# Turn of layers in a two-layer decoder: order of one evacuation on ScalarE, order of products in a layer's last pair

## The chip, the core and the metric

The kernel runs on one core of a Trainium2 chip. Five engines work side by side, each through its own list of instructions in order: TensorE (PE; its weight loads are shown as PEld), VectorE (DVE), ScalarE (ACT), GpSimd (POOL) and SyncE (SP). They wait for each other through semaphores. PE writes to PSUM, which has eight banks of 128 partitions by 512 float32; the other tiles lie in SBUF. DMAs are issued by SP, POOL and ACT. The metric is the device time of one execution in microseconds (us), the median of several.

## The reference

A decoder trunk of two layers on 512 tokens of 1024 features, all in float32. Each layer mixes (attention over a sliding window beside a retention branch, both gated) and then applies an MLP; the change lies where the MLP of the first layer ends and the second layer begins, and in the MLP's up projection.

```python
def hybrid_layer(x, g_mix, w_in, sinks, w_a, w_b, w_out, g_mlp, w_up, w_down):
    h = rmsnorm(x, g_mix)
    z = h @ w_in
    ...
    x = x + mixed @ w_out

    h2 = rmsnorm(x, g_mlp)
    x = x + jnp.square(jax.nn.relu(h2 @ w_up)) @ w_down
    return x
```

`w_up` is 1024 x 4096, `w_down` 4096 x 1024, `w_in` 1024 x 5888. A final rmsnorm follows the second layer.

## The kernel before

**Products.** A float32 product is made of three products in a rounded float32 format (fp32r): each operand is split into a high part (ACT copies it to fp32r) and a low part (DVE subtracts), and `products` (lines 391 to 393) issues hi·hi, hi·lo and lo·hi. Weights come by SP's queue in units of 128 x 1024 (`raw`), and `split_until` splits them (line 339 on ACT, 340 on DVE) up to three units ahead of their use. In the group that opens the second layer `by_halves` (line 406) issues the same products in another order: all with a unit's high weights, then all with its low weights, then the high weights with the low parts of x.

**The MLP.** The 4096 inner features are taken in eight blocks of 512 (`e` = 0 to 7). A block's up projection is two *pairs* (only block 0 is made otherwise), its down projection is `down` (in the last block of the last layer `down_plain`). Both `pair` and `down` use a block scheme with seven products in place of eight. `pair(which)` computes 256 inner features for 512 tokens; it holds three PSUM banks: a, e and b. Its steps, with their lines:

- a takes four times three products of x's first quarter (line 391 to 393, shown as `mm<-xh,hi` and so on);
- `nc.scalar.activation(b, a, AF.Copy)`, line 1343: ACT copies a into bank b, on which b's products then accumulate;
- e takes twelve products of the first sum (`sums[0]`, shown as `mm<-r,hi`), line 1344; ACT copies it to `eu`, line 1345;
- b goes on with `sums[1]`, is copied to `eu` (1348); a goes on and is evacuated through Relu into `z` (1350); b with `sums[2]` and e with x's last quarter meet `eu` on DVE (1355, 1357); b with `sums[3]` ends in `z` (1363).

Block 7 of the first layer thus has two pairs in a row, 28 pairs stand in the whole program, and the pool `ps_mm` that gives their banks has five. `down` takes four banks of it and two of the second pool, `ps_aux` (b).

**The end of a layer.** `down` writes its results through an object `into`. For blocks 0 to 6 that is `Adding`, which adds to the tensor `y` in DRAM by accumulating DMAs. For block 7 it is `Ending`: it loads `y` back into SBUF and adds the last block there. The layer's output has two token halves, i = 0 and 1. For i = 0 DVE adds from PSUM (`add`). For i = 1 in the first layer `join` does it: ACT evacuates PSUM to a temporary `eu` (line 1515) and a POOL DMA adds it to the tile `y` (line 1516). The last of these four joins is (j, m) = (0, 1); it is the last result of `down`, from bank b.

**The turn.** `y` has tokens on the partitions, x has features there, so the sum is transposed on PE (`turn`, line 1554), four 128 x 128 transposes for a tile, and DVE adds it to x (line 1560). `last_but_one` does the half i = 0, that is x chunks 0 to 3, and splits each chunk with the next layer's gain (`scaled_input`, line 414 on ACT and 415 on DVE). `carry` does i = 1, x chunks 4 to 7, which needs the joins. `squares` squares all eight chunks for the next rmsnorm (ACT, lines 546 and 549; DVE adds, 550; PE sums over the partitions, 562) and stores x to DRAM (`spill`, line 1595, SP's queue). `carry` and `squares` are called from within the first `group` of the second layer, after the high-weight products of its second unit.

**What sets the order.** The program is written through a scheduler (`schedule_with_timeline_sim=True`): when the program is built, it lays out each engine's list by a simulated timeline. Of the instructions that are ready there, the one that stands earlier in the program goes first; tiles and banks are given out in the same pass. On the chip the lists are fixed. `tc.issue_after(ins)` adds to what is written in its block, on the engine of `ins` alone, that it stands behind `ins` in that list; it makes nothing wait for the end of `ins`. `latest[0]` is the last matrix product written so far.

Of the kernel before, what the change touches and what calls it, by code (L numbers as in the profile page):

```python
# [12 lines left out]
AF = mybir.ActivationFunctionType  # L13
# [31 lines left out]
N_BLOCK = 8  # L45
# [70 lines left out]
def decoder(ctx, tc, xT, x_first, w_in, w_rv, w_a, w_b, w_out, w_up, w_pair, w_down, w_end, tables, decay, band, g_last, out):  # L116
    nc = tc.nc
# [13 lines left out]
    def temp(name="t"):  # L131
        return tmp.tile([P, T], F32, tag="t", name=name, bufs=7)

    def big(name, dtype=F32):
        return tmp.tile([P, 2, T], dtype, tag="big", name=name, bufs=6)

    def bank(pool, name):
        return pool.tile([P, T], F32, tag=pool.name, name=name)
# [212 lines left out]
    def unit(name, layer):  # L351
        i = state["next"]
        assert order[i][:2] == (layer, name), (order[i], layer, name)
        state["next"] += 1
        hold = state["hold"]
        split_until(i + SPLIT + 1 if hold is None else max(i + 1, min(hold, i + SPLIT + 1)))
        return parts.pop(i)
# [27 lines left out]
    def products(ps, pairs, start, stop, resume=False):  # L385


        n = len(pairs)
        for i, ((ah, al), (bh, bl)) in enumerate(pairs):
            more = {"skip_group_check": True} if resume else {}  # L390
            nc.tensor.matmul(ps, ah, bh, start=start and i == 0, stop=False, **more)  # L391
            nc.tensor.matmul(ps, ah, bl, start=False, stop=False, **more)  # L392
            latest[0] = nc.tensor.matmul(ps, al, bh, start=False, stop=stop and i == n - 1, **more).ins  # L393

    latest, behind = [None], []
# [148 lines left out]
    def square_sum(acc, src, first):  # L544
        if first:
            nc.scalar.activation(acc, src, AF.Square)
        else:
            sq = temp("sq")
            nc.scalar.activation(sq, src, AF.Square)
            nc.vector.tensor_tensor(acc, acc, sq, ALU.add)  # L550
# [28 lines left out]
    def squared_input(k, which):  # L579
        if k == 0:  # L580
            acc_of[which] = tmp.tile([P, T], F32, tag="acc", name="acc", bufs=1)
        square_sum(acc_of[which], x[:, k, :], k == 0)
# [32 lines left out]
    def layer_body(layer):  # L615
        g_mix, g_mlp = 2 * layer, 2 * layer + 1
# [516 lines left out]
        for u in range(4):  # L1133
            hi, lo = unit("w_a", layer)
            for j in range(2):
                c = 2 * u + j
                ps = bank(ps_mm, "mm")
# [90 lines left out]
        sums = Forms((0, 2))  # L1228
# [47 lines left out]
        def block(half, tokens):  # L1276
            at = slice(tokens * H, tokens * H + H)
            return [(xh[:, k, at], xl[:, k, at]) for k in range(4 * half, 4 * half + 4)]
# [27 lines left out]
        def second_rest(z):  # L1306
            if not kept:
                return
            kept.pop()
            u_forms.rest(0, z, (3,))  # L1310
# [15 lines left out]

            return put

        def pair(which):
            def multiply(ps, weights, left, moving, start=True):  # L1330
                hi, lo = weights
                cols = [slice((0 if left else 4 * P) + k * P, (0 if left else 4 * P) + (k + 1) * P) for k in range(4)]
                products(ps, [((hi[:, c], lo[:, c]), m) for c, m in zip(cols, moving)], start, True, not start)

            a, e, b = (bank(ps_mm, "mm")[:, :H] for _ in range(3))
            eu, z = temp("eu"), big("z")  # L1340
            part = unit("pair", layer)
            multiply(a, part, True, block(0, 0))
            nc.scalar.activation(b, a, AF.Copy)  # L1343
            multiply(e, part, False, sums[0])
            nc.scalar.activation(eu[:, :H], e, AF.Copy)
            part = unit("pair", layer)
            multiply(b, part, True, sums[1], False)
            nc.scalar.activation(eu[:, H:], b, AF.Copy)
            multiply(a, part, False, block(1, 0), False)
            nc.scalar.activation(z[:, 0, :H], a, AF.Relu)  # L1350
            if which:
                second(z, slice(0, 1), SOON)
            part = unit("pair", layer)
            multiply(b, part, True, sums[2], False)
            nc.vector.scalar_tensor_tensor(z[:, 1, H:], b, -1.0, eu[:, :H], ALU.mult, ALU.subtract)
            multiply(e, part, False, block(1, 1), False)
            nc.vector.tensor_tensor(z[:, 0, H:], e, eu[:, H:], ALU.add)
            nc.scalar.activation(z[:, :, H:], z[:, :, H:], AF.Relu)
            if which:
                second_late(z)  # L1360
            part = unit("pair", layer)
            multiply(b, part, True, sums[3], False)
            nc.scalar.activation(z[:, 1, :H], b, AF.Relu, scale=-1.0)
            if which:
                second(z, slice(1, 2), SOON)
                second_rest(z)
            elif plain:
                first_plain(z)
            else:
                first_two(z)  # L1370
# [119 lines left out]
        class Ending:  # L1490
# [21 lines left out]

            def join(self, i, j, m, ps, scale):
                t = temp("eu")
                nc.scalar.activation(t, ps, AF.Copy, scale=scale)
                nc.gpsimd.dma_start(self.y[i, j, m], t, accum_op=ALU.add)

            def add(self, i, j, m, ps, scale, at=slice(0, T)):
# [3 lines left out]
            def put(self, i, j, m, ps, sign, at=slice(0, T)):  # L1522
                block = 2 * j + m
                scale = (factor if sign > 0 else negative)[:, block : block + 1]
                if i and not last:
                    self.join(i, j, m, ps, scale)
                    return
                with tc.issue_after(self.queued) if i else ExitStack():
                    self.add(i, j, m, ps, scale, at)
                if last:  # L1530
                    v = self.y[i, j, m]
                    first, total, both = (sq[:, n * NB + block : n * NB + block + 1] for n in range(3))
                    nc.scalar.activation(temp("junk")[:, at], v[:, at], AF.Square, accum_out=both if i else first)
                    if not i:
                        nc.vector.tensor_tensor(v, v, last_gain[:, i, :], ALU.mult)
                        self.queued = nc.vector.tensor_scalar(first, first, 1.0 / D, EPS, ALU.mult, ALU.add).ins
                        return
                    if at.stop < T:
                        nc.vector.scalar_tensor_tensor(first, both, 1.0 / D, first, ALU.mult, ALU.add)
                        return  # L1540
                    nc.scalar.activation(total, both, AF.Sqrt, bias=first, scale=1.0 / D)
                    nc.vector.reciprocal(total, total)
                    nc.vector.scalar_tensor_tensor(v, v, total, last_gain[:, 1, :], ALU.mult, ALU.mult)
                    nc.sync.dma_start(out[:, block, T:], v)
                    v = self.y[0, j, m]
                    nc.scalar.activation(v, v, AF.Copy, scale=total)
                    nc.scalar.dma_start(out[:, block, :T], v)
# [18 lines left out]
            def last_but_one(self):  # L1566
                if not last:
                    for half in range(2):
                        for j in range(2):
                            turned = self.turn(0, j, half, ps_mm)  # L1570
                        for k in (2 * half, 2 * half + 1):
                            self.behind = scaled_input(k, g_mix + 2)
                        if half == 0:
                            self.turned = turned
                            behind.append(self.behind)
                    behind.append(self.behind)

# [13 lines left out]

            def squares(self):
                for k in range(KD):
                    squared_input(k, g_mix + 2)
                    nc.sync.dma_start(spill[:, k, :], x[:, k, :])

        def first_hooks():
# [16 lines left out]
        for e in range(N_BLOCK):  # L1614
            if e == 0:
                into = Adding(e)
                hooks = first_hooks()
                for c in (0, 2):
                    two_chunks("w_up", layer, xs, [put_up(c), put_up(c + 1)], hooks[c // 2])
            else:  # L1620
                plain = last and e == N_BLOCK - 1
                into = Ending() if e == N_BLOCK - 1 else Adding(e)
                pair(0)
                pair(1)
            if last and e == N_BLOCK - 1:
                down_plain(into)
            else:
                down(e, into)
# [177 lines left out]
```

## Time and profile before

| | |
|---|---|
| time, median of 3 runs | 1468.51 us (1467.56 to 1468.66) |
| the profiled execution | 1466.77 us |
| its span, first to last instruction | 1465.0 us |
| PE busy, of the span | 1453.4 us, 99% |
| DVE busy | 1124.7 us, 77% |
| ACT busy | 944.6 us, 64% |
| POOL busy | 209.0 us, 14% |
| granted TensorE clock | 0.999 |
| DMA | 287.32 MB, 196 GB/s on average |

The profile is of one execution. A row of its timeline has the start in us from the span's beginning, the duration, the engine (a q behind it means its queue), the line of the kernel, the operation, what it writes and reads (`out<-in`), the shapes, and how many like instructions were merged; brackets give the idle time of the engine before it and who ended that. Matrix products overlap: one of 512 columns is shown with 0.39 us though the next starts 0.23 us later. A wait for several semaphores is put down to the one that came last. The row "DMA to landing" gives the time from a DMA's issue until its data is there, as minimum, median and maximum of those in the window that was asked.

### The profile page before, as it was taken

To read this page: it belongs to the slowest core of one execution; us is meant where nothing else is said; L and a number is where in the kernel's file an instruction comes from. 1 tells how busy PE (TensorE), PEld (TensorE's weight loads), DVE (VectorE), ACT (ScalarE), POOL (GpSimd) and SP (SyncE) were. 2 spreads that over 40 slices of the span, in tenths; PEclk is the share of its full clock that TensorE was granted. 3 is DMA by queue.
4 is the path that set the end of the run, shared out by engine and by line. 5 is a ranking of instruction groups with operands and counts; after the bars stand their busy time and mean duration, and the time that the engine had idled before them with its cause. 6 is when DMAs were issued, how large, how long until landed. Compare 5 with 4: busy or idle time off the path is not lost.

```text
span 1465.0 us, 21388 instructions
## 1 busy us (share of the span) xinstructions
PE 1453.4 (99%) x7751; PEld 1256.2 (86%) x7751; DVE 1124.7 (77%) x1697; ACT 944.6 (64%) x1549; POOL 209.0 (14%) x302
## 2 busy tenths in 40 slices
PE   9999999999999999999999999999999999999998
PEld 7888888888889999999878888888888899999996
DVE  6978877866677888888878688787757678888885
ACT  7657556543467777777756575565435777777775
POOL 0111001112001111112201110012110111111120
PEclk9999999999999999999999999999999999999999
DMA  7597349689815767666956973597793377777664
GB/s 263 182 295 207 114 152 259 200 207 290 228 57 193 195 188 199 181 172 188 297 172 191 291 212 104 181 251 189 228 272 101 99 197 199 196 189 199 180 186 140
DMA packets 95867, 287.32 MB, mean 196 GB/s; under 512 B 11152, under 2 KB 11280, under 8 KB 90896
## 3 DMA queue, kind: packets, MB, share of 16 engines
q0 software_dynamic: 33648, 113.26, 34.3%
q1 hardware_dynamic: 61392, 171.37, 33.5%
q8 instruction: 61, 1.00, 0.3%
q10 hardware_dynamic: 720, 1.31, 0.2%
q14 instruction: 46, 0.38, 0.1%
HBM read 246.05 MB, written 107.48 MB: 241 GB/s over the span
## 4 chain that ended last, share of the span: by engine, by line
PE 97%; DMA 1%; ACT 1%; DVE 0%; issue 0%; SPq 0%; DVEq 0%; ACTq 0%
PE mm L391 25%; PE mm L393 25%; PE mm L392 25%; PE b L391 3%; PE b L392 3%; PE b L393 3%; PE rv L391 2%; PE rv L392 2%; PE rv L393 2%; PE mm L406 1%; PE score L774 1%; PE pT L739 1%; PE r L393 1%; PE r L392 1%; PE r L391 1%; DMA y<-eu 1%
## 5 line engine op out<-in xcount | busy, mean ns | idle before, releaser
L339 ACT ACTIVATE hi<-raw 128x1024 fp32r<-128x1024 f32 (+1 forms) x375 | 382.3, 1020 | 285.3 <-PE mm L392 166.0
L340 DVE TENSOR_TENSOR lo<-raw,hi 128x1024 fp32r<-128x1024 f32 (+1 forms) x376 | 439.2, 1174 | 144.6 <-ACT hi L339 143.2
L391 PE MATMUL mm<-xh,hi 128*128 128x512 f32 (+1 forms) x976 | 344.1, 355 | 1.0 <-ACT xh L414 1.0
L392 PE MATMUL mm<-xl,hi 128*128 128x512 f32 (+1 forms) x976 | 344.0, 355 | 0.0
L393 PE MATMUL mm<-xh,lo 128*128 128x512 f32 (+1 forms) x976 | 341.9, 355 | 0.0
L393 PE MATMUL mm<-r,lo 128*128 128x256 f32 (+1 forms) x736 | 239.2, 325 | 0.5 <-DVE lo L340 0.5
L392 PE MATMUL mm<-r,hi 128*128 128x256 f32 (+1 forms) x736 | 239.3, 325 | 0.0
L391 PE MATMUL mm<-r,hi 128*128 128x256 f32 (+1 forms) x736 | 236.6, 325 | 0.5 <-ACT mm L1343 0.5
L391 PEld LDWEIGHTS mm<-xh,hi 128*128 128x128 f32 x976 | 184.8, 189 | 25.6 <-ACT xh L414 1.4
L392 PEld LDWEIGHTS mm<-xl,hi 128*128 128x128 f32 x976 | 184.9, 189 | 24.2
L393 PEld LDWEIGHTS mm<-xh,lo 128*128 128x128 f32 x976 | 183.9, 189 | 23.6
L391 PEld LDWEIGHTS mm<-r,hi 128*128 128x128 f32 x736 | 139.9, 190 | 13.7 <-ACT mm L1343 0.7
L392 PEld LDWEIGHTS mm<-r,hi 128*128 128x128 f32 x736 | 139.9, 190 | 13.2
L393 PEld LDWEIGHTS mm<-r,lo 128*128 128x128 f32 x736 | 139.9, 190 | 12.1 <-DVE lo L340 0.7
L1488 POOL DMA_DIRECT2D y<-eu x56 | 62.4, 1358 | 369.1 <-DVE eu L1473 369.1
L392 PE MATMUL mm<-lo,r 128*128 128x512 f32 (+1 forms) x276 | 104.4, 388 | 0.0
L393 PE MATMUL mm<-hi,r 128*128 128x512 f32 (+1 forms) x276 | 101.2, 387 | 0.0
L391 PE MATMUL mm<-hi,r 128*128 128x512 f32 (+1 forms) x276 | 98.7, 391 | 0.5 <-ACT r L411 0.2
L391 PE MATMUL b<-hi,r 128*128 128x512 f32 x180 | 70.5, 392 | 0.0
L392 PE MATMUL b<-lo,r 128*128 128x512 f32 x180 | 70.3, 391 | 0.0
L393 PE MATMUL b<-hi,r 128*128 128x512 f32 x180 | 67.9, 390 | 0.0
L1488 POOL DMA_DIRECT2D y<-y x56 | 55.6, 1007 | 78.7 <-ACT y L1483 73.5
(299 smaller groups left out, 2382.3 us busy)
## 6 DMA issues: line engine op xcount, KB each, us to landing
raw<-w_in_in SPq DMA_DIRECT2D x73, 512.0 KB, 4.8
sums_down<-w_down_in POOLq DMA_DIRECT2D x30, 1024.0 KB, 11.1
sums_up<-w_pair_in POOLq DMA_DIRECT2D x56, 512.0 KB, 10.2
raw<-w_down_in SPq DMA_DIRECT2D x45, 512.0 KB, 6.8
raw<-w_pair_in SPq DMA_DIRECT2D x84, 256.0 KB, 3.7
y<-y POOLq DMA_DIRECT2D x62, 256.0 KB, 9.0
y<-eu POOLq DMA_DIRECT2D x62, 256.0 KB, 8.1
raw<-sums_down SPq DMA_DIRECT2D x30, 512.0 KB, 7.1
```

The lines of the kernel that those rows point to most:

```text
L339: state["high"] = nc.scalar.activation(hi[:, at], raw[:, at], AF.Copy).ins
L340: nc.vector.tensor_tensor(lo[:, at], raw[:, at], f32(hi[:, at]), ALU.subtract)
L391: nc.tensor.matmul(ps, ah, bh, start=start and i == 0, stop=False, **more)
L392: nc.tensor.matmul(ps, ah, bl, start=False, stop=False, **more)
L393: latest[0] = nc.tensor.matmul(ps, al, bh, start=False, stop=stop and i == n - 1, **more).ins
L406: latest[0] = nc.tensor.matmul(ps, w[:, cols(j, c)], moving[k][low], start=first, stop=bool(final)).ins
L739: nc.tensor.transpose(pt[:, i * P : (i + 1) * P], sm[:, at : at + P], ident)
L774: nc.tensor.matmul(ps[:, g * w : (g + 1) * w], q_s[g][:, c, at], part[:, keys], start=i == 0, stop=i == 1)
L1488: nc.gpsimd.dma_start(y[:, 2 * j + m, i * T : (i + 1) * T], t, **how)
```

## The change

Three edits.

In `pair`, the twelve products of e are written ahead of the copy b<-a, in all 28 pairs. In the second pair of block 7, in both layers, e's products stand behind a's last product in PE's list.

In `Ending`, `join` remembers its evacuation; the last join, (0, 1) of i = 1, is queued on ACT behind `self.ahead`, which is the high part of x chunk 1 (line 414, the first half of `last_but_one`).

In `squares`, each squaring is queued on ACT behind the last join's evacuation. The stores to DRAM beside it stay as they are.

```diff
-        def pair(which):
+        def pair(which, ordered=False):
...
             multiply(a, part, True, block(0, 0))
+            with tc.issue_after(latest[0]) if ordered else ExitStack():
+                multiply(e, part, False, sums[0])
             nc.scalar.activation(b, a, AF.Copy)
-            multiply(e, part, False, sums[0])
             nc.scalar.activation(eu[:, :H], e, AF.Copy)
...
             def join(self, i, j, m, ps, scale):
                 t = temp("eu")
-                nc.scalar.activation(t, ps, AF.Copy, scale=scale)
+                self.joined = nc.scalar.activation(t, ps, AF.Copy, scale=scale).ins
                 nc.gpsimd.dma_start(self.y[i, j, m], t, accum_op=ALU.add)
...
                 if i and not last:
-                    self.join(i, j, m, ps, scale)
+                    with tc.issue_after(self.ahead) if (j, m) == (0, 1) else ExitStack():
+                        self.join(i, j, m, ps, scale)
                     return
...
                             self.turned = turned
+                            self.ahead = self.behind[0]
                             behind.append(self.behind)
...
             def squares(self):
                 for k in range(KD):
-                    squared_input(k, g_mix + 2)
+                    with tc.issue_after(self.joined):
+                        squared_input(k, g_mix + 2)
                     nc.sync.dma_start(spill[:, k, :], x[:, k, :])
...
                 pair(0)
-                pair(1)
+                pair(1, e == N_BLOCK - 1)
```

## The prediction

> **What bounds the kernel now.** I read the page first: span, busy time, the chain that ended last.
>
> ```profile
> span 1465.0 us, 21388 instructions
> PE 1453.4 (99%) x7751; PEld 1256.2 (86%) x7751; DVE 1124.7 (77%) x1697; ACT 944.6 (64%) x1549; POOL 209.0 (14%) x302
> PE 97%; DMA 1%; ACT 1%; DVE 0%; issue 0%; SPq 0%; DVEq 0%; ACTq 0%
> ```
>
> TensorE (PE) is busy for 99% of the span and holds 97% of the chain. The diff adds and removes no matrix product, so it can gain only what PE stands idle, and lose only by new idle time. The view of waits, for PE alone, lists all of it that a wait explains:
>
> ```profile
> PE turn L1554 <- DMA y<-eu: 1.2, 1, 1.2
> PE warm L371 <- DVE ones L366: 1.1, 1, 1.1
> PE mm L391 <- ACT xh L414: 1.0, 1, 1.0
> PE mm L393 <- DVE lo L340: 0.5, 1, 0.5
> PE mm L391 <- ACT mm L1343: 0.5, 1, 0.5
> PE mm L391 <- ACT r L411: 0.2, 1, 0.2
> ```
>
> That is about 4.5 us (1.2+1.1+1.0+0.5+0.5+0.2); the second and third lie in the start (the warm-up and the first products). The diff touches the places of the first, the fifth and the sixth row, and no other. So this is a change of one to three microseconds at best, unless it makes new stalls. 0.2% of the median, 2.94 us, is about what a measurement of this kernel can tell from no change.
>
> **The turn of layers.** The timeline of ScalarE (ACT) and PE, from the last products of layer 0 on (columns: start, duration, engine, line, operation; in brackets the idle time before):
>
> ```profile
> 727.72 0.40 PE L393 MATMUL b<-hi,r 128*128 128x512 f32 x1
> 727.32 1.34 ACT L414 ACTIVATE xh<-x 128x512 fp32r<-128x512 f32 x2 [1.18 <-DVE x L1560]
> 728.56 1.05 ACT L339 ACTIVATE hi<-raw 128x1024 fp32r<-128x1024 f32 x1
> 729.51 0.61 ACT L546 ACTIVATE acc<-x 128x512 f32<-128x512 f32 x1
> 730.03 0.67 ACT L1515 ACTIVATE eu<-b,columns 128x512 f32<-128x512 f32 x1
> 731.05 0.85 POOL L1516 DMA_DIRECT2D y<-eu  x1 [3.71 <-ACT eu L1515]
> 735.47 0.82 PE L1554 MATMUL turn<-ident,y 128*128 128x128 f32 x6
> 736.04 1.63 PE L406 MATMUL mm<-xh,lo 128*128 128x512 f32 x6
> 738.83 0.87 PE L1554 MATMUL turn<-ident,y 128*128 128x128 f32 x6 [1.16 <-DMA y<-eu]
> DMA to landing us min/median/max: 7.7/7.7/7.7
> DMA to landing us min/median/max: 4.6/4.6/4.6
> ```
>
> The last product into the joined block b ends at 728.12 (727.72 + 0.40). ACT is free at 728.66, but then runs a weight split (L339) and the first square (L546), and evacuates b only at 730.03. The accumulating DMA is issued at 731.05 and lands 7.7 us later (first landing row), at about 738.8. PE takes six transposes at 735.47, six products, and waits 1.16 us for that landing. The last row is the landing of the join's DMA before it, issued at 726.5: 4.6 us.
>
> The diff queues the squares behind this evacuation, and the evacuation behind the split of x chunk 1, the second of the two L414 at 727.32. It has no edge for the weight split; its description says that the evacuation goes ahead of one. So the evacuation moves up by 0.52 us (730.03 − 729.51, the square alone) to 1.47 us (730.03 − 728.56, both). I take 1.47, for the evacuation stands earlier in the program than that split and b is complete 0.54 us before ACT is free. With it moves the one DMA that it feeds (L1516); POOL had been idle 3.71 us before it, so it passes nothing in that queue. SP's queue has no part in it: the spill writes read x, not the squares.
>
> What is late next costs nothing, by these rows:
>
> ```profile
> 730.25 1.22 DVE L340 TENSOR_TENSOR lo<-raw,hi 128x1024 fp32r<-128x1024 f32 x1
> 733.65 1.98 PE L406 MATMUL mm<-xh,hi 128*128 128x512 f32 x8
> 747.88 1.49 DVE L550 TENSOR_TENSOR acc<-acc,sq 128x512 f32<-128x512 f32 x2
> 754.14 0.95 PE L562 MATMUL ssq<-ones,acc 128*128 128x1 f32 x8
> ```
>
> The split and the square start about 0.6 us later (the evacuation's 0.67 less overlap). The split ends by 730.3 instead of 729.61, and PE uses that second weight unit from 733.65 on: 3 us of cover. The sum of squares is complete at 749.37 and is read at 754.14: 4.8 us of cover. Were that cover gone, each would cost the 0.6 us.
>
> What the earlier landing is worth: issued at 729.58, the DMA lands at 734.2 with the 4.6 us of its neighbour, at 737.3 with its own 7.7 us. PE comes to the waiting transposes at 737.67 (736.04 + 1.63) in today's order; the order is written when the program is built, so it may put them up to the six products (1.63 us) earlier, at 736.04. In most of these pairings landing comes before arrival, so the 1.16 us go; I count **1.2 us**. Bounds: 0 (landing at 737.3 with arrival at 736.04 leaves 1.26 us, as much as now) and 1.4, counted by starts (738.83 − 736.04, less six steps of 0.23).
>
> [...]
>
> **The last pair of layer 0.** Second pair, block 7:
>
> ```profile
> 694.64 1.06 ACT L339 ACTIVATE hi<-raw 128x1024 fp32r<-128x1024 f32 x1 [1.99 <-PE mm L392]
> 696.02 0.37 ACT L1343 ACTIVATE mm<-mm 128x256 f32<-128x256 f32 x1 [0.33 <-PE mm L393]
> 696.30 0.38 ACT L1350 ACTIVATE z<-mm 128x256 f32<-128x256 f32 x1
> 701.90 0.37 ACT L1345 ACTIVATE eu<-mm 128x256 f32<-128x256 f32 x1
> 695.71 0.28 PE L393 MATMUL mm<-xh,lo 128*128 128x256 f32 x1
> 696.44 0.39 PE L391 MATMUL mm<-r,hi 128*128 128x256 f32 x1 [0.46 <-ACT mm L1343]
> 696.67 0.28 PE L392 MATMUL mm<-r,hi 128*128 128x256 f32 x1
> 705.05 0.28 PE L393 MATMUL mm<-xh,lo 128*128 128x256 f32 x1
> 705.51 0.50 PE L391 MATMUL mm<-hi,r 128*128 128x512 f32 x1 [0.18 <-ACT r L411]
> 705.85 0.39 PE L392 MATMUL mm<-lo,r 128*128 128x512 f32 x1
> ```
>
> The copy b<-a (L1343) starts the moment a's products end, and PE waits for it with b's products: from 695.71 to 696.67 there are 0.96 us where two steps of 0.12 would do (1425.28 to 1425.40 in the last fence), so **0.72 us** lost. e's products, which need nothing from ACT, came later: their evacuation (L1345) is at 701.90. The five PSUM banks explain it: the pair before holds three, a the fourth, and the copy, first in the program, the fifth; e waited for the bank that L1350 empties at 696.30. The diff puts e's products before the copy in the program (all 28 pairs) and, in the last pair of each layer, behind a's on PE. Then e holds the fifth bank and its twelve products (12 × 0.12 = 1.44 us) cover the copy, if L1350 empties a bank for it in time: L1350 and L1343 together are 0.75 us. Bounds: 0.72 gained, or 0.72 lost once more if L1350 is queued behind a's end; I take 0.72, as ACT idles 1.99 us just before.
>
> Moving e's products forward also brings the twelve products behind them nearer. At 705.51 the down stage waits for the split of the first pair's result, from 705.05 to 705.85: 0.80 where 0.12 + 0.23 would do (six 512-column products in 1.63 us at 736.04, the last one 0.4 long, step by 0.23 to 0.25), **0.45 us**. PE would arrive there 0.72 us earlier, but the result of the first pair is finished up to 1.44 us earlier; I count the 0.45 as gone, bounds 0 and 0.45.
>
> In the last layer the same pair has no gap: a's last product at 1425.28, the next at 1425.40, the copy beside it. There, and in the other pairs, the copy was covered already, so I cost the edit at nothing:
>
> ```profile
> 1425.28 0.28 PE L393 MATMUL mm<-xh,lo 128*128 128x256 f32 x1
> 1425.40 0.28 PE L391 MATMUL mm<-r,hi 128*128 128x256 f32 x1
> 1425.69 0.36 ACT L1343 ACTIVATE mm<-mm 128x256 f32<-128x256 f32 x1
> 574.79 0.36 ACT L1350 ACTIVATE z<-mm 128x256 f32<-128x256 f32 x1
> 578.36 0.36 ACT L1343 ACTIVATE mm<-mm 128x256 f32<-128x256 f32 x1
> ```
>
> **Sum.** 1.2 + 0.72 + 0.45 = 2.37 us off. The profiled execution took 1466.77 us, its span 1465.0 and 1.77 around it; the span becomes 1462.6. The median of the runs, 1468.51, lies 1.74 above that execution, so I forecast 1468.51 − 2.37 = 1466.1 us.
>
> **Rivals.**
> 1. *The turn keeps its wait.* The planner moves the transposes forward with the evacuation, and landing and arrival shift alike. For it: bounds above meet at 1.26 us. Against it: a quieter neighbour lands in 4.6. Only the pair's 1.17 us remain: 1467.3.
> 2. *The change does not do what it says*: other work takes the slot on ACT, the pair's bank is late; the order of PE stays as it is: 1468.5.
> 3. *The landing does not move* (slower). If traffic and not issue decides the 738.8, and the transposes are planned 1.63 us earlier, PE stands from 736.04 to 738.83, 2.8 us instead of 1.4; with the pair's gain lost too, 1469.9. It decides from a transfer of 9.2 us (738.8 − 729.58) on; the longest of the join's rows is 7.7.
> 4. *The bank* (slower). If in the other second pairs too b's copy gets its bank only after e's products, each loses the 0.72 us: 14 × 0.72 = 10.1, less 1.2 at the turn, 1477.4. It decides when L1343 starts over 1.44 us after a's end. Against it: at block 3 L1350 empties a bank at 574.79, 3.2 us before the copy (578.36 − 575.15).
> 5. *More falls away*: planned anew, layer 1 loses its 0.5 us wait (fourth row of waits) as well: 1465.5 or below.
>
> **How the numbers follow.** Forecast 0.46, rivals 0.20, 0.09, 0.07, 0.12 and 0.06 in order. The runs of before differ by 1.1 us (1467.56 to 1468.66), so about a quarter of the forecast's share falls beyond −2.94 us: faster 0.11 + 0.06 = 0.17; slower 0.12, the bank alone; same the remaining 0.71. The range goes from 1465.0 (rival 5 and half the scatter) to 1470.0 (rival 3) and leaves out the bank and a few hundredths.
>
> **What would show it.** Right: the L1515 at the turn directly behind the two L414 and ahead of L546; its DMA landing before PE comes to the second transposes; no entry for L1554, L1343 or that L411 in PE's waits; L1345 of layer 0's last pair near 697.5. Wrong: PE's wait on the join's DMA still over 1 us (rival 1 or 3), a new wait of PE on L1343 in several pairs (rival 4), or new PE waits in layer 1, whose order is planned anew from the turn on; that last is what I can price least.

## The result, and the profile after

The changed kernel took 1473.45 us (median, 1470.51 to 1474.58) beside 1468.03 us (1466.12 to 1468.87) for the kernel before on the same chip: 1.0037 times as long, 95% interval 1.0024 to 1.0050. It is slower, by about 5 us; 1466.1 us had been forecast.

The page of the changed kernel. Its execution took 1474.58 us, 7.8 us more than the 1466.77 us of before's:

```profile
span 1472.8 us, 21340 instructions
...
PE 1457.5 (99%) x7751; PEld 1258.8 (85%) x7751; DVE 1122.7 (76%) x1697; ACT 943.5 (64%) x1549; POOL 208.8 (14%) x302
...
PE 97%; ACT 1%; DMA 1%; DVE 0%; issue 0%; SPq 0%; DVEq 0%; ACTq 0%
```

PE has the same 7751 products, yet is "busy" for 4.1 us longer: some of them ran slower. The rest is waiting. PE's waits follow (what it waited for, total, times, longest). Lines behind the edits have numbers one to four higher than before: L1343 is L1345, L1345 is L1346, L1515 is L1516, L1554 is L1556.

```profile
PE mm L406 <- ACT xh L414: 2.7, 1, 2.7
PE mm L393 <- DVE lo L340: 1.8, 1, 1.8
PE warm L371 <- DVE ones L366: 1.1, 1, 1.1
PE mm L391 <- ACT r L411: 1.0, 2, 0.8
PE mm L391 <- ACT eu L1346: 0.9, 1, 0.9
PE mm L391 <- ACT xh L414: 0.8, 1, 0.8
```

Against before: the wait on the join's DMA (1.2) is gone, as forecast. New is 2.7 us at the turn, where PE waits for ACT's split of x (L414). L340 grew by 1.3, L411 by 0.8 (one wait of 0.81 us at 1449.75, in the last layer), and 0.5 on the copy became 0.9 on e's evacuation; the wait in the start is 0.2 shorter. That is 3.8 us. The two places where products ran slower are in the windows (busy time and count of each engine; the last three columns are PEclk, DMA share, GB/s). Before:

```profile
6.00:8.00 2.00, 2.00 (x11) 1.63 (x10) 2.00 (x4) 2.00 (x5) 0.00 (x0) 1.00 0.92 319
8.00:10.00 2.00, 2.00 (x11) 1.65 (x10) 2.00 (x5) 2.00 (x5) 0.00 (x0) 1.00 1.05 388
...
735.00:740.00 5.00, 3.84 (x23) 3.02 (x22) 4.40 (x6) 1.34 (x2) 0.00 (x0) 1.00 0.97 304
```

After:

```profile
6.00:8.00 2.00, 2.00 (x6) 1.52 (x6) 2.00 (x4) 1.77 (x4) 0.00 (x0) 1.00 0.95 309
8.00:10.00 2.00, 2.00 (x6) 1.60 (x5) 1.84 (x4) 1.75 (x4) 0.00 (x0) 1.00 1.05 406
...
730.00:735.00 5.00, 2.33 (x10) 1.72 (x9) 4.26 (x6) 2.71 (x4) 0.45 (x1) 0.88 0.96 265
735.00:740.00 5.00, 5.00 (x18) 4.03 (x18) 4.75 (x6) 5.00 (x9) 0.40 (x1) 0.78 0.92 270
```

At the turn the granted clock falls: 5 x 0.12 + 5 x 0.22 = 1.7 us lost. In windows of 1 us it stands at 0.50 from 734 to 737. In the start six products pass in 2 us where eleven did before, in two rows: ten fewer, at 0.227 us each 2.3 us. Together 3.8 + 1.7 + 2.3 = 7.8 us, all of it. The start is not the change's: PE's list is the same up to about 458 us, and a second profile of the changed kernel (e5, below) has the start as before.

**The turn.** First PE before, around its transposes of the first token half:

```profile
720.46 0.40 PE L393 MATMUL mm<-hi,r 128*128 128x512 f32 x1
720.70 0.60 PE L1554 MATMUL turn<-ident,late 128*128 128x128 f32 x4
...
725.25 1.47 PE L1554 MATMUL turn<-ident,late 128*128 128x128 f32 x12
```

Then PE, DVE and ACT after:

```profile
725.30 0.62 PE L393 MATMUL mm<-hi,r 128*128 128x512 f32 x2
...
728.25 0.40 PE L393 MATMUL b<-hi,r 128*128 128x512 f32 x1
728.49 1.91 PE L1556 MATMUL turn<-ident,late 128*128 128x128 f32 x16
733.06 3.20 PE L406 MATMUL mm<-xh,hi 128*128 128x512 f32 x8 [2.67 <-ACT xh L414]
...
725.73 1.41 DVE L1521 SCALAR_TENSOR_TENSOR late<-mm,columns,late 128x512 f32<-128x512 f32 x2 [0.94 <-PE mm L393]
729.23 0.69 DVE L1562 TENSOR_TENSOR x<-x,turn 128x512 f32<-128x512 f32 x1 [2.09 <-PE turn L1556]
729.84 1.22 DVE L340 TENSOR_TENSOR lo<-raw,hi 128x1024 fp32r<-128x1024 f32 x1
730.97 1.88 DVE L1562 TENSOR_TENSOR x<-x,turn 128x512 f32<-128x512 f32 x3
...
732.28 1.34 ACT L414 ACTIVATE xh<-x 128x512 fp32r<-128x512 f32 x2 [4.28 <-DVE x L1562]
733.53 0.67 ACT L1516 ACTIVATE eu<-b,columns 128x512 f32<-128x512 f32 x1
734.10 1.05 ACT L339 ACTIVATE hi<-raw 128x1024 fp32r<-128x1024 f32 x1
```

Before, four transposes went right behind another bank's last product (720.46), eighteen products of b followed, then the other twelve transposes and six more products of b to cover the sums and splits. After, all sixteen stand behind b's last product (728.25): nothing is left to run while DVE adds and ACT splits, and PE stands idle for 2.67 us. Part of that time DVE spends on a weight split (L340 at 729.84, 1.22 us) between its first add to x and the other three; before, the split (727.20) came behind the first three adds. No run moved this split alone, so its share of the gap is not shown. The eight products at 733.06 take 3.20 us where seven steps of 0.227 and the last one's 0.39 would make 2.0. The join's evacuation (L1516 at 733.53) is where the diff says, right behind the two L414 and ahead of L339.

### The profile page after: what moved, and what is told of

The parts are those of the page before. It is cut to its first block, busy times and chain, and to the rows that moved or that the text cites. A ratio compares the mean times of both kernels' runs of the same rounds, so it can differ in the third digit from the quotient of the medians.

```text
span 1472.8 us, 21340 instructions
## 1 busy us (share of the span) xinstructions
PE 1457.5 (99%) x7751; PEld 1258.8 (85%) x7751; DVE 1122.7 (76%) x1697; ACT 943.5 (64%) x1549; POOL 208.8 (14%) x302
## 4 chain that ended last, share of the span: by engine, by line
PE 97%; ACT 1%; DMA 1%; DVE 0%; issue 0%; SPq 0%; DVEq 0%; ACTq 0%
PE mm L391 25%; PE mm L392 25%; PE mm L393 25%; PE b L391 3%; PE b L392 3%; PE b L393 3%; PE rv L393 2%; PE rv L391 2%; PE rv L392 2%; PE mm L406 2%; PE score L774 1%; PE pT L739 1%; PE r L393 1%; PE r L392 1%; PE r L391 1%; DMA raw<-sums_up 0%
## 5 line engine op out<-in xcount | busy, mean ns | idle before, releaser
L339 ACT ACTIVATE hi<-raw 128x1024 fp32r<-128x1024 f32 (+1 forms) x375 | 383.0, 1022 | 292.3 <-PE mm L392 185.8
L340 DVE TENSOR_TENSOR lo<-raw,hi 128x1024 fp32r<-128x1024 f32 (+1 forms) x376 | 439.5, 1174 | 158.4 <-ACT hi L339 157.3
```

The lines of the kernel that those rows point to most:

```text
L339: state["high"] = nc.scalar.activation(hi[:, at], raw[:, at], AF.Copy).ins
L340: nc.vector.tensor_tensor(lo[:, at], raw[:, at], f32(hi[:, at]), ALU.subtract)
```

## The experiments

Each kernel was run beside the kernel before on the same chip. Times are medians in us; the ratio has its 95% interval. The largest wait is PE's in each profile, start and the wait on L340 apart.

| run | time | before | ratio | largest wait of PE |
|---|---|---|---|---|
| e1 turn's edits alone | 1466.40 | 1466.54 | 1.0000 (0.9991 to 1.0008) | 0.46, block 7 |
| e2 pairs' edits alone | 1480.98 | 1466.54 | 1.0096 (1.0082 to 1.0110) | 6.36 at 861; turn 2.66 |
| e3 b in the other pool | 1471.60 | 1466.54 | 1.0038 (1.0024 to 1.0052) | 3.49, block 7 |
| e4 last pairs and turn | 1469.90 | 1466.54 | 1.0020 (1.0011 to 1.0030) | 1.79, block 7 |
| e5 the change again | 1473.10 | 1466.91 | 1.0039 (1.0027 to 1.0052) | 2.66, turn |
| e6 transposes sooner | 1470.57 | 1466.91 | 1.0026 (1.0016 to 1.0035) | 1.28, turn |
| e7 gap filled | 1469.08 | 1466.91 | 1.0018 (1.0010 to 1.0027) | 0.88, block 7 |
| e8 last pair, second layer | 1466.77 | 1466.91 | 0.9999 (0.9990 to 1.0008) | 0.81, last `down` |
| e9 all but last pairs | 1472.57 | 1466.62 | 1.0030 (1.0019 to 1.0042) | 2.25, block 7 |
| e10 no pin | 1472.78 | 1466.62 | 1.0040 (1.0027 to 1.0054) | 2.66, turn |
| e11 transposes first | 1471.36 | 1466.62 | 1.0029 (1.0017 to 1.0040) | 1.21, turn |
| e12 last pair, first layer | 1468.89 | 1466.62 | 1.0012 (1.0004 to 1.0021) | 1.79, block 7 |
| e13 not in blocks 7 | 1467.08 | 1466.98 | 0.9998 (0.9989 to 1.0008) | 0.46, block 7 |
| e14 second layer only | 1468.72 | 1466.98 | 1.0011 (1.0002 to 1.0020) | 0.81, last `down` |

"Block 7" is that of the first layer. The medians of the kernel before lie between 1466.54 and 1468.03, and the speed of the first products, which changes by execution (last section), moves single profiles by about 2 us. So profiles with the same start are compared too.

### Which part of the diff

Theory A put the loss on the pairs' edit and the shortage of banks, its variant A2 on e's move in every pair; theory B put it on the evacuation that is queued behind the split of x.

e1, the turn's edits without the pairs':

```diff
-            with tc.issue_after(latest[0]) if ordered else ExitStack():
-                multiply(e, part, False, sums[0])
-            nc.scalar.activation(b, a, AF.Copy)
+            with ExitStack():
+                nc.scalar.activation(b, a, AF.Copy)
+            multiply(e, part, False, sums[0])
```

> The edits at the turn alone; the copy b<-a stands ahead of e's products as in the kernel before. The lists of all engines are then those of before but for one swap on ACT: the last join's evacuation ahead of the first square (not ahead of the weight split). Theory A (the pairs' order costs the time): PE's wait for the join's DMA falls from 1.16 us by the square's 0.52 to about 0.6, no other new wait; ratio to before 0.999 to 1.000. Theory B (queueing the evacuation behind the split of x costs the time): 3 us or more lost at the turn, ratio 1.002 or above.

1.0000: no loss, and no gain that can be measured. Its ACT and PE:

```profile
730.68 1.05 ACT L339 ACTIVATE hi<-raw 128x1024 fp32r<-128x1024 f32 x1
731.64 0.67 ACT L1516 ACTIVATE eu<-b,columns 128x512 f32<-128x512 f32 x1
732.20 0.62 ACT L546 ACTIVATE acc<-x 128x512 f32<-128x512 f32 x1
...
740.22 0.87 PE L1556 MATMUL turn<-ident,y 128*128 128x128 f32 x6 [0.41 <-DMA y<-eu]
```

The evacuation passes the square only, not the weight split: 0.52 us of the 1.47 I had taken. Its DMA took 7.5 us (before 7.7). So the wait shrinks by 0.75 us, to 0.41, and does not go.

e2, the pairs' edits without the turn's:

```diff
-                    with tc.issue_after(self.ahead) if (j, m) == (0, 1) else ExitStack():
+                    with ExitStack():
                         self.join(i, j, m, ps, scale)
...
-                    with tc.issue_after(self.joined):
+                    with ExitStack():
                         squared_input(k, g_mix + 2)
```

> e's products ahead of the copy in all pairs, and behind a's in the last ones; the turn's edits are out. Theory A: PE idle of 0.9 us in block 7's last pair and of about 2.7 us at the turn stay, ratio as with the whole change, 1.0025 to 1.005. Theory B: the 2.7 us at the turn go, since the evacuation no longer waits for the split of x; ratio below 1.002.

Much slower still. The 2.66 us at the turn are there without any of the turn's edits, behind the same sixteen transposes, so B falls. What e2 loses beyond the changed kernel is in the second layer (the rows from 840.85 on):

```profile
726.52 1.91 PE L1556 MATMUL turn<-ident,late 128*128 128x128 f32 x16
731.10 3.49 PE L406 MATMUL mm<-xh,hi 128*128 128x512 f32 x8 [2.66 <-ACT xh L414]
...
840.85 0.33 SPq L195 DMA_DIRECT2D raw<-w_a_in  x1
841.23 0.61 SPq L626 DMA_DIRECT2D rawtab<-tables_in  x1
...
858.83 1.23 DVE L627 TENSOR_TENSOR tab<-rawtab,rstd 128x1024 f32<-128x1024 f32 x1 [8.04 <-DMA rawtab<-tables_in]
...
860.94 0.76 PE L391 MATMUL mm<-xh,hi 128*128 128x512 f32 x1 [6.36 <-DVE rot L636]
```

A table load (L626) is issued at 841.23, right behind a weight load in SP's list; before it was issued at 825.39. DVE waits 8.04 us for its data, and PE 6.36 us for DVE.

e3, b of the first layer's last pair in the second pool of banks, so that the copy needs no bank of e's pool:

```diff
-            a, e, b = (bank(ps_mm, "mm")[:, :H] for _ in range(3))
+            a, e, b = (bank(pool, "mm")[:, :H] for pool in (ps_mm, ps_mm, ps_aux if ordered and not last else ps_mm))
```

> The whole change, but in the last pair of the first layer b lies in a bank of the second pool, so the copy needs no bank that the Relu of the pair before must empty first. Theory A: PE's wait of 0.9 us in that pair goes, the pair's results come some 2 us earlier, products of b stand behind the turn's transposes again, and the idle at the turn falls from 2.7 us to under 1; 3 to 4 us of the loss go, ratio 0.9995 to 1.0015. Theory B: the turn keeps its 2.7 us, ratio 1.003 or above.

The loss stays. The wait in the pair goes, as A expected, and PE no longer waits at the turn for more than 0.2 us. But it now waits 3.49 us in front of `down` in block 7 (for r L411): with other banks the lists are laid out anew, and the stall has moved.

e4 has e moved in the last pairs of both layers only, with the turn's edits; e12 in the first layer's last pair alone (`ordered and not last` in place of `ordered`); e8 in the second layer's alone (`ordered and last`). The diff is e4's:

```diff
+            if not ordered:
+                nc.scalar.activation(b, a, AF.Copy)
             with tc.issue_after(latest[0]) if ordered else ExitStack():
                 multiply(e, part, False, sums[0])
-            nc.scalar.activation(b, a, AF.Copy)
+            if ordered:
+                nc.scalar.activation(b, a, AF.Copy)
```

> The turn's edits, and e's products ahead of the copy in the last pair of each layer alone; the other 26 pairs as before. Theory A: the wait in block 7's last pair stays near 0.9 us or less, as the bank is short there alone; how much of the turn's 2.7 us stays depends on how many of b's products stand behind the transposes (12 here, none in the changed kernel), I expect under 1 us; ratio 0.9995 to 1.0015. A rival A2 (moving e costs in every pair): this one is as fast as before within 0.5 us and the changed kernel's loss lies spread over the blocks. Theory B: 1.003.

> The turn's edits, and e's products ahead of the copy only in the last pair of the first layer (pinned there as in the changed kernel). The run with both last pairs moved had 1.79 us of PE idle in this pair, on a DVE instruction (L1359 there) that stands behind two weight splits, 0.88 us before it, and 0.81 us before the last down stage. Theory T: the first two are this pair's and stay, the third goes back to 0.13 us; about 0.7 us under that run's 1469.9, so 1469.2. Rival: the pair's waits are scatter and go; 1466.5 to 1467.

> The turn's edits as in the changed kernel, and e's products ahead of the copy only in the last pair of the second layer (twelve lines of PE's list differ from the kernel with the turn's edits alone). Theory T: everything as with the turn's edits alone but the wait on r L411 in front of the last down stage, 0.81 us in all four profiles with that pair moved, 0.13 us in the two without; so 0.6 to 0.8 us slower than the kernel with the turn's edits alone, whose median was 1466.4: 1467.1. Rival: the 0.7 us is made up behind it (the last stage is short of other work), 1466.4 and the same as before.

The waits of e4 and e12 in block 7 are alike: both have 0.88 us on e's evacuation and 1.79 us on DVE, 2.0 us more than before's 0.46 and 0.18. PE in e12:

```profile
707.71 0.39 PE L391 MATMUL mm<-r,hi 128*128 128x256 f32 x1 [1.79 <-DVE z L1359]
```

The wait before the last `down` is 0.81 us in e4 and 0.13 in e12, and e12's 1468.89 us lie near the 1469.2 expected. At the turn PE waits 0.5 us in e4 and 0.2 in e12, in place of 1.2. So e4 lay above what A expected, and by another wait as well, the 1.79 us on DVE. A2 had e4 within 0.5 us of before, and it falls too. e12 shows more: with the edit only in the one pair whose wait on the copy was to go (and the turn's edits, which cost nothing in e1), the kernel is slower (1.0012). e8's trace has the 0.81 us; its time does not show it, and with an interval 0.0018 wide it could not.

### The order at the turn, and the clock

Theory T: the loss is the order that PE's list has at the turn, and the clock that falls behind the gap. e5 is the changed kernel again.

> The changed kernel once more, so that the next two runs have it beside them. Theory T (the order of the turn, and the clock behind it): PE's list has all sixteen transposes of the first token half behind b's last product, so PE idles about 2.67 us at the turn for the split of x (L414) and then runs some 3.4 us of products at half the granted clock, 1.7 us more; both are properties of the list and come again, idle within 0.1 us. Median 1472 to 1475 us. Rival S (scatter of one execution): the idle at the turn or the low clock behind it is gone in this profile. The wait on lo L340 near 1188 us was 1.82 us in the first profile and 0.31 to 0.72 us in five others; T takes it for scatter of DMA landings and expects under 1 us here, a rival that counts it to the change expects 1.5 us or more.

e5's profile took 1471.01 us; its start is before's, its wait on L340 0.4 us, its wait at the turn 2.66 us again. So 4.2 of the first profile's 7.8 us (1471.01 − 1466.77) come again. The other 3.6 are the start (about 2.3) and the wait on L340 (1.4), which differ here for the same lists. The medians differ by more, 5.4 and 6.2 us, and this execution was the second fastest of its five. What the other one to two microseconds of the medians are is not shown; the start and the wait on L340 may be part of them. Its windows at the turn, where the clock falls again:

```profile
730.00:735.00 5.00, 4.17 (x13) 3.31 (x14) 4.09 (x7) 4.95 (x8) 0.85 (x1) 0.73 0.95 329
735.00:740.00 5.00, 5.00 (x23) 4.03 (x22) 4.75 (x6) 4.18 (x6) 0.00 (x0) 0.93 0.82 223
```

e6 queues half of b's last twelve products behind the transposes, e11 all twelve (`and m` left out); `self.crossed` is the last transpose of `turn`:

```diff
-                    products(ps[m], pairs, start, True, not start)
+                    with tc.issue_after(behind) if behind and m else ExitStack():
+                        products(ps[m], pairs, start, True, not start)
...
-            multiply(b, u_forms[3], False)
+            multiply(b, u_forms[3], False, getattr(into, "crossed", None))
```

> The changed kernel with one edit: b's last six products (its second half, m = 1) are queued on PE behind the transposes of the first token half. The built lists differ from the changed kernel's on PE alone, by ten transposes that move ahead of six products of b. Theory T: x is summed and split 1.36 us earlier (six steps of 0.227), PE's idle at the turn shrinks from 2.67 to about 1.3 us, the granted clock stays 1.00 (a gap of 1.79 us between products left it at 1.00 in the run with only the last pairs moved), and the time falls by 2.5 to 3.5 us against the changed kernel of this call. Rival Q (the cost is the join's evacuation queued behind the split of x): the evacuation stays where it is, gain 0.5 us or less. Rival M (the cost is e's products ahead of the copy in 28 pairs): gain 0.5 us or less.

As expected: 2.5 us faster than e5 by the medians, 2.6 by the profiles (1468.38 and 1471.01), with ten transposes in another place on PE. PE and the clock:

```profile
724.96 1.25 PE L1557 MATMUL turn<-ident,late 128*128 128x128 f32 x10
...
727.44 0.82 PE L1557 MATMUL turn<-ident,late 128*128 128x128 f32 x6
729.53 1.66 PE L406 MATMUL mm<-xh,hi 128*128 128x512 f32 x6 [1.28 <-ACT xh L414]
```

```profile
730.00:735.00 5.00, 5.00 (x24) 4.12 (x23) 4.21 (x7) 5.00 (x9) 0.85 (x1) 1.00 1.06 324
```

The gap is 1.28 us and the clock stays at 1.00.

> As the run with the transposes sooner, but all twelve of b's last products are queued behind the transposes; the lists differ from the changed kernel's on PE alone, ten transposes ahead of twelve products. Theory T: the chain late add on DVE (L1521), transpose, add to x, split (L414) sets when products on x can start. In the run with six behind it left 1.28 us of idle; with twelve behind, the transposes come to the front before the late adds are done, so PE waits some 1.2 to 1.4 us for DVE there in place of the wait on L414, x starts within 0.4 us of that run, granted clock 1.00, and the time is that run's 1470.6 within 0.6 us. Rival (PE's own order is all that counts): the idle goes altogether and the time falls by another 1.3 us, to 1469.3.

No further gain, as T had it; 1471.36 is 0.8 us above e6, a little more than the 0.6 allowed. The wait did not move as a whole: there are 0.62 us on the late add (L1522 there) and still 1.21 us on L414, as six transposes remained behind all twelve products. As I read it, late add, transpose, add to x and split are a chain that PE's order can't shorten; it can only lay work beside it.

e7 keeps the order and fills the gap: sixteen more transposes that change no value.

```diff
-                for k in range(2):
+                for k in range(2 * (5 if (i, j, half) == (0, 1, 1) else 1)):
+                    k = k % 2
```

> The changed kernel with the transposes of the last tile of the first token half done five times in place of once (sixteen more transposes, 1.74 us of PE work that changes no value) in the gap in which PE waits for the split of x. Theory T: the products on x start no earlier than before, within 0.4 us of the changed kernel's, but PE's idle is under 1.3 us, so the clock is not taken down: granted clock 1.00 throughout and the time 1.3 to 1.8 us below the changed kernel of this call. Rival S (the clock falls for another reason) or transposes that do not count as work for the clock: clock again about 0.8 over 735 to 740 us, time the same or up to 0.5 us longer. The list of PE behind the second transposes differs by some twenty lines from the changed kernel's, so 0.5 us either way is open.

```profile
725.95 3.65 PE L1557 MATMUL turn<-ident,late 128*128 128x128 f32 x32
729.93 1.42 PE L406 MATMUL mm<-xh,hi 128*128 128x512 f32 x5 [0.32 <-ACT xh L414]
```

```profile
730.00:735.00 5.00, 5.00 (x22) 4.15 (x23) 4.61 (x7) 5.00 (x8) 0.85 (x1) 1.00 1.00 328
```

Idle work made the kernel faster: 4.0 us by the medians, 2.7 by the profiles (1468.27 and 1471.01), where 1.3 to 1.8 had been expected. From the transposes' start to the products on x are 3.98 us (e5: 726.26 to 730.83, 4.57), 0.6 less than in e5; 1.7 of the other 2.1 are the clock, which is now 1.00. The changed kernel's first profile has 0.78 us from ACT's first L414 to the products (732.28 and 733.06); by my estimate from that, x starts sooner because this L414 comes right behind DVE's second add to x (at about 729.15; that add ends at 729.13), in e5 behind the third (at about 730.05). So the gain is not the clock's alone. By the medians e7 is still 2.2 us slower than before.

e10 leaves the pin out (`with ExitStack():` in place of `tc.issue_after(latest[0]) if ordered`).

> The changed kernel without the pin of e's products behind a's last one in the last pairs; nothing else (in the built lists two products of e per layer move by some twenty places on PE, the other four engines' lists are equal). Theory T: the order of the turn is the changed kernel's, so PE idles 2.66 us there and runs at half clock behind it; time within 0.7 us of the changed kernel's 1473.1. Rival O (the pin itself costs, by making PE wait in the pair): 1471.5 or less.

1472.78, and the same 2.66 us: the pin has no part in it that these runs show.

### Does each moved pair pay?

e9 has e moved in all pairs but the last of each layer (e4's diff with `ordered` negated), with the turn's edits.

> The turn's edits, and e's products ahead of the copy in all pairs but the last of each layer (those two are as before). Theory T: in these 26 pairs the edit moves work but costs nothing on PE; the built list has sixteen transposes with twelve products of b behind them, so no idle over 0.6 us at the turn, granted clock 1.00 there, and the wait on r L411 before the last down stage is 0.13 us as before. Between 1466.4 (the turn's edits alone) and 1467.4, since the changed kernel shows 0.3 to 0.5 us of small new steps in the second layer. Rival M (each pair pays something for the bank, or the stalls are spread): 1469 or more.

Missed by 5 us; by its time alone rival M would be right. The turn is free of stalls, but block 7 is not:

```profile
708.08 0.39 PE L391 MATMUL mm<-xh,hi 128*128 128x256 f32 x1 [2.25 <-ACT eu L1349]
```

```profile
705.00:710.00 5.00, 2.75 (x19) 2.55 (x19) 4.39 (x6) 4.53 (x9) 0.00 (x0) 0.91 1.06 349
710.00:715.00 5.00, 5.00 (x25) 4.36 (x24) 3.72 (x7) 3.92 (x7) 1.68 (x2) 0.75 0.83 299
```

That is 2.25 us of wait, and 5 x 0.09 + 5 x 0.25 = 1.7 us of clock. PE waits for e's evacuation (L1349 at 707.66), which stands on ACT behind a weight split (L339 at 705.75, 1.06 us) and a squaring (L1283, 1.04 us). Theory U: the edit is free where another block's products stand ready, and the loss is made where block 7 of the first layer and the turn are laid out anew. e13 moves e in the 24 pairs of blocks 1 to 6, e14 in the fourteen pairs of the second layer:

```diff
-            with tc.issue_after(latest[0]) if ordered else ExitStack():
+            moved = number < N_BLOCK - 1
+            if not moved:
+                nc.scalar.activation(b, a, AF.Copy)
+            with tc.issue_after(latest[0]) if ordered and moved else ExitStack():
                 multiply(e, part, False, sums[0])
-            nc.scalar.activation(b, a, AF.Copy)
+            if moved:
+                nc.scalar.activation(b, a, AF.Copy)
```

(`number` is the block's. e14 has `moved = last`.)

> The turn's edits, and e's products ahead of the copy in the pairs of blocks 1 to 6 of both layers (24 of 28); the four pairs of the two blocks 7 as before. The built list of PE differs from that with the turn's edits alone by 492 lines in those blocks, but has block 7 of the first layer and the turn in the old order (4 transposes, 18 products of b, 12 transposes, 6 products of b). Theory U (the edit is free wherever other blocks' products stand ready; the loss is made where block 7 of the first layer and the turn are laid out anew): PE waits at the turn as with the turn's edits alone (0.5 us or less on the join's DMA), 0.46 us on the copy in block 7, no granted clock under 1.00 after the start, 0.13 us before the last down stage: 1466.4 to 1467.2. Rival M (each moved pair pays): 24/28 of the 6 us, some 1471 to 1472.

> The turn's edits, and e's products ahead of the copy in the fourteen pairs of the second layer alone, its last pair pinned as in the changed kernel. The built lists of the first layer and the turn are those with the turn's edits alone. Theory U: no new wait but the 0.81 us before the last down stage in place of 0.13 and 0.3 us or less of new steps near 1188 and 1290 us; 0.7 to 1.0 us over the turn's edits alone, 1467.1 to 1467.4. Rival M: half of the changed kernel's loss, 1469.5 or more.

e13 equals before within its interval: 24 moved pairs cost nothing that it can tell, and rival M falls. At the turn it has before's order, four transposes and then twelve. e9 moves two pairs more, the first ones of the two blocks 7, and is some 5 us slower; its stall lies in the first layer's. No run moves that pair alone. e14's profile has the 0.81 us at the end and 0.51 us at the turn, and no other new wait. But its interval (1.0002 to 1.0020) lies above 1, and its median is 1.3 us above what U said: what the second layer's pairs cost beyond the 0.7 us at the end stays open.

No version beat the kernel before by more than the runs can tell.

## Why the prediction was wrong

**The step that failed** is in the turn: "PE comes to the waiting transposes at 737.67 (736.04 + 1.63) in today's order". I let the planner shift six products and took the rest of PE's list from the trace of before. But the pairs' edit changes the program order in 28 places, and PE's list is another from about 458 us on, far ahead of the turn. With it all sixteen transposes came behind b's last product: 2.67 us of wait and 1.7 us of clock, against 1.2 us saved. The same slip stands at the head of the sum: "The diff touches the places of the first, the fifth and the sixth row, and no other." That the pairs' edit alone does this e2 shows; that these two terms are the larger part of the loss e6 and e7 show, which still stand 3.7 and 2.2 us above before by the medians. Only runs with both pairs of that block moved have no product of b behind the sixteen transposes (e2, e5, e7 and e10). With one of the two moved (e9, e12), or with the other bank (e3), twelve products of b follow the transposes; PE has no stall on the split of x at the turn, and loses in block 7. The danger was among the signs of being wrong ("new PE waits in layer 1, whose order is planned anew from the turn on"), too late in the program and without a price; and no rival carried it, so "slower" got 0.12 for the bank alone.

**The turn's 1.2 us** came true in the changed kernel, by luck and not by the mechanism: there is no wait on the join's DMA, whose transfer took 4.1 us, because PE comes to the last transposes later (742.08; the data landed at 738.7). The evacuation did not come sooner: it starts 4.9 us behind b's last product, where before it started 1.9 us behind. Alone (e1) the edit moved it by 0.52 us, the lower end of my range, and 0.41 us of the wait stayed. That traffic makes the 7.7 us out of the neighbour's 4.6, as rivals 1 and 3 take it, no run shows; in before the DMAs moved 172 to 220 GB/s in the 2 us windows from 726 to 732 us and 311 to 402 in those from 732 to 738.

**The last pair's 0.72 us** failed: "Then e holds the fifth bank and its twelve products cover the copy". ACT and PE after:

```profile
699.66 0.63 ACT L339 ACTIVATE hi<-raw 128x512 fp32r<-128x512 f32 x1 [1.53 <-PE mm L392]
700.20 0.37 ACT L1346 ACTIVATE eu<-mm 128x256 f32<-128x256 f32 x1
700.47 0.38 ACT L1351 ACTIVATE z<-mm 128x256 f32<-128x256 f32 x1
700.87 0.37 ACT L1345 ACTIVATE mm<-mm 128x256 f32<-128x256 f32 x1
...
699.47 0.28 PE L393 MATMUL mm<-r,lo 128*128 128x256 f32 x1
700.62 0.39 PE L391 MATMUL mm<-xh,hi 128*128 128x256 f32 x1 [0.88 <-ACT eu L1346]
```

e's products do run at once, and then the next group waits for ACT to evacuate e (L1346), which stands behind a weight split. 0.46 us on the copy became 0.88 us on the evacuation. My lower bound had a late bank in it, the one that L1350 empties; here it was the evacuation of e, one instruction further on. **The 0.45 us** at `down` did go: L411's waits no longer have one there.

**"I cost the edit at nothing"** in the other pairs: right within e13's interval for 24 of them. It was wrong for the last pair of the second layer, where e8 and all runs with that pair moved show 0.81 us on L411 in place of 0.13, and, by e9 beside e13, wrong for the first pairs of the blocks 7, where the loss is some 5 us (together with the 24; no run moves them alone). Rival 4, the bank, is out: no wait on the copy in any other pair, and another bank (e3) does not help.

**The size**: a profile with before's start (e5) is 4.2 us longer, and its waits and clock account for that: 2.7 + 1.7 − 1.2 at the turn, 0.2 net in the pair, 0.7 at the end, 4.1. The medians lose 5.4 and 6.2 us; what the rest is stays open. So does why the planner preferred b's products to the transposes, which is not in the trace.

## What to carry to other kernels

Where a planner orders the whole program, price an edit on its new lists, not on the trace of the old ones: an edit in a repeated helper moves work far from itself, and the harm shows where, as I read these runs, nothing stands ready to fill a gap, here the last block of the first layer. Weigh a gap in front of PE by its length: here gaps of 2.25 us and more cost 1.7 us or more of clock as well (e9, after, e3, e2), gaps up to 1.81 us did not, and with idle work in the gap (e7) the kernel took 4.0 us less than with the gap (e5), by the medians. And follow a removed wait to the next instruction that waits: the wait on the copy was in one pair of 28, and moving e in that pair alone (e12) put two longer waits in its place (0.46 us before, 0.88 and 1.79 us in e12).

## What the hardware showed that I had not expected

**The clock behind a gap.** These are gaps of PE in the profiles, and the lowest granted clock in the 5 us windows around (how low depends on where the window falls): 1.16 (before), 1.28 (e6) and 1.79 us (e12), 1.00; 2.25 us (e9), 0.75; 2.67 us (after), 0.78; 3.49 us (e3), 0.66; 6.36 us (e2), 0.54. The 1.81 us on L340 in the first profile after left it at 1.00 too (windows of 2 us from 1184 to 1194). Behind the 2.67 us the windows of 1 us from 733 to 738 read 0.89, 0.50, 0.50, 0.50 and 0.90: 1.7 us lost, by my estimate from these five about 3.4 us at half clock. No gap between 1.81 and 2.25 us is among these, so where the fall begins is not shown.

**The start.** The same first products run at about 11 (before) or at 6 (the first profile after) in 2 us until about 10 us, by the execution. From 6 to 12 us 27 or 28 products pass in the faster profiles, 18 to 21 in the slower: against before's 28 that is 1.6 to 2.3 us, at 0.227 us each. The changed kernel had both, the slower in its first profile and the faster in e5; of the sixteen profiles five had the slower (the first one after, e1, e3, e9 and e14). The granted clock reads 1.00 in both, so this column does not show it, and the cause is open. A comparison of single profiles of this kernel has to begin with the first 10 us.

**A wait that follows no edit.** PE's wait on L340 near 1180 us was between 0.3 and 1.8 us over thirteen profiles (all but those of e6 to e8), 1.8 and 0.4 for the same lists (after, e5).
